# Rows of values by head, spread over the partitions as two rounded parts in place of one fp32 product

## The chip, the cores and the metric

The kernel runs on one core of a Trainium2 chip. The time is device microseconds of that core, the median of the runs shown. TensorE is called PE below (its weight loads PEld), VectorE DVE, ScalarE ACT, GpSimd POOL, SyncE SP. "Rounded" means the type fp32r: an fp32 word that TensorE takes in a shortened form. A number that is to keep its precision is then carried as two rounded words, the rounded value ("hi") and the rest ("lo").

## The reference, cut to what matters

One layer of a trunk with three parallel branches (a gated linear recurrence, gated linear attention, GLA, and an mLSTM), a merge, an output projection and a squared-ReLU MLP, for 256 prompt tokens and 8 samples of 4 tokens. The two groups are computed together: 288 columns of tokens. Three places of it concern this change; each has a number per head and token that acts on all features of the head:

```python
y_gla = rmsnorm(o.astype(dt), P['gla_g_norm']).reshape(...) * jax.nn.silu(g_gate)      # 4 heads, 256 features each
...
inter = F + m[..., None]                                                               # mLSTM, running maximum
mt = jnp.maximum(inter, jnp.max(Dm, axis=-1))
W = jnp.exp(Dm - mt[..., None])
...
y_ml = jax.nn.sigmoid(m_o) * rmsnorm(h.astype(dt), P['ml_g_norm']).reshape(B, T, MLSTM_WIDTH)
```

In the first and the last, the factor 1/sqrt(mean of squares) of a head multiplies that head's features. In the second, a running maximum of a head is subtracted within the decay matrix of the prompt part.

## The kernel before, in words

Features lie on the 128 partitions and tokens along the free axis. Every large product streams its weights: a tile of 128x1024 words comes from memory by a transfer that SP issues (`fetch`, L155), ACT rounds it into `hi` (L164), DVE subtracts to get `lo` (L171), and PE multiplies with it (`stream_`, L197 to L199): three rounded products for each 128x128 block of weights, hi by the activation's hi, hi by its lo, lo by its hi. A tile holds eight blocks, so it feeds 24 products of 128x288. There are three buffers each for the raw tile, for `hi` and for `lo`; ACT can round a new tile once PE has left the `hi` buffer that it goes into.

Beside these streams, generators called "sides" carry the branches: `run` (the loop over a stream) lets each side take one step after every weight tile. A tile scheduler with a time model then sets the order of the instructions on each engine (only SP's is by hand); code under `high_priority` is moved ahead of other work that is ready. Each engine executes its own instructions in the order so made.

A quantity per head is kept as a row block: head h stands on partitions 32h to 32h+31, all 32 alike. To let it act on a head's features it must be spread over all 128 partitions. `head_bcast` (L128) does that with one fp32 product: the stationary operand is one column of the identity, `ident[:, 32h]`, repeated 128 times, the moving operand is the row block, and the result in a PSUM tile `px` (there are two such buffers) holds row 32h on every partition. It is used in these places:

- `gla`, at the end: `inv_sqrt` makes `sums` (L498 to L502: transpose on DVE, square root on ACT, reciprocal and transpose on DVE), and for each head `scaled_rows` spreads it (L128), multiplies two blocks of features by it on DVE (L918) and splits the result into hi (ACT, L542) and lo (DVE, L543). This runs beside the stream over the mLSTM's input projection (`to_slot`, L584, evacuates that stream on ACT).
- `mlstm`, for each head: the running maximum `mr` of the 256 prompt tokens is spread, and DVE uses it from PSUM (L1406). The neighbours on PE are fp32 products (L1412, L1415).
- `mlstm`, at the end: as in `gla`, with L1582 (a gate) ahead of L918. The results `y` are the activations of the stream over `wbm`, where PE names them `s`.
- `mlstm`, once more, for 32 columns (x8 in the trace): this use stays as it is.

The kernel already has the other form in one place: `parts` (L877 to L882) rounds its source on ACT, subtracts on DVE and multiplies both parts with rounded selectors.

Of the kernel before, what the change touches and what calls it, by code (L numbers as in the profile page):

```python
# [8 lines left out]
F32 = mybir.dt.float32  # L9
F32R = mybir.dt.float32r  # L10
AF = mybir.ActivationFunctionType
ALU = mybir.AluOpType
# [41 lines left out]
def trunk(ctx, tc, io):  # L54
# [18 lines left out]
    def nm(s):  # L73
        uid[0] += 1
        return f"{s}_{uid[0]}"

    def slot(i, dt=F32):
        return big.tile([P, 8, N], dt, tag=f"s{i}", name=nm(f"s{i}"))
# [33 lines left out]
    def row(n):  # L112
        return sp.tile([P, N], F32, tag=f"r_{n}", name=nm("row"), bufs=1)
# [11 lines left out]
    def head_bcast(p, r, w=N):  # L125

        def f(h):
            T.matmul(p[:, 0:w], ident[:, 32 * h:32 * h + 1].to_broadcast([P, P]), r[:, 0:w], start=True, stop=True)  # L128
        return f


# [781 lines left out]
    def scaled_rows(y, z, r, h):  # L913

        p = misc()
        head_bcast(p, r)(h)
        a = slice(2 * h, 2 * h + 2)
        V.tensor_tensor(out=z[:, a], in0=z[:, a], in1=p[:, :N].unsqueeze(1).to_broadcast([P, 2, N]), op=ALU.mult)  # L918
        split(y[0][:, a], y[1][:, a], z[:, a])
# [6 lines left out]
        V.tensor_copy(dst[:, 2 * h:2 * h + 2, NP:N], p[:, 0:2 * NS].rearrange("p (e t) -> p e t", e=2))  # L926

    def gla():
        kk_, g_cs, ee = slot(3), slot(4), slot(5)
        wg2 = flat(kk_)[:, 4 * N:4 * N + 512]  # L930
        G.dma_start(wg2, io["wg2"])
# [193 lines left out]
        def result(h):  # L1125
            if h == 0:
                y.extend([slot(8, F32R), slot(3, F32R)])
            scaled_rows(y, sg, sums, h)

        at = {}  # L1130

        def do(s, f, *a):
            at.setdefault(s, []).append(lambda: f(*a))
# [17 lines left out]
            do(4 * h + 7, squares, h)  # L1151
            do(22 + h, result, h)
        do(20, head_sums, sums, oT)
        do(21, lambda: inv_sqrt(sums, sums, bias=eps, scale=1.0 / 256))
        yield from steps(at)
        ygla.extend(y)

# [135 lines left out]
    def mlstm():  # L1293
# [101 lines left out]
        psb = by_head(sc([P, P], "gks", 1), psb)  # L1395

        nT = slot(0)
        den = row("lf")
        cst = None
        ws = {}  # L1400
        for h in range(4):
            p = misc()
            head_bcast(p, mr, NP)(h)
            w0, w1 = ws[h] = [e0[:, 384 * h + a:384 * h + b] for a, b in ((0, 256), (256, 384))]
            for t, w in ((0, w0), (1, w1)):
                V.tensor_scalar(w, p[:, t * P:256], col[:, t, h:h + 1], 0.0, ALU.subtract, ALU.max)  # L1406
                S.activation(w, w, AF.Exp, scale=-1.0)
                V.tensor_tensor(out=w[:, 0:P], in0=w[:, 0:P], in1=C("causal"), op=ALU.mult)
            p = misc()
            for e in range(2):  # L1410
                n = 2 * h + e
                T.matmul(p[:, 0:256], mc[:, n, 0:P], tf[:, n, 0:NP], start=e == 0, stop=e == 1)  # L1412
            for e in range(2):
                n = 2 * h + e
                T.matmul(p[:, 256:384], mc[:, n, P:NP], tf[:, n, P:NP], start=e == 0, stop=e == 1)  # L1415
            V.tensor_tensor(out=w0, in0=w0, in1=p[:, 0:256], op=ALU.mult)
            V.tensor_tensor(out=w1, in0=w1, in1=p[:, 256:384], op=ALU.mult)
            yield
            if h % 2 == 0:
                cst = sp.tile([P, 1028], F32, tag="st", name=nm("st"), bufs=2)  # L1420
            for d in range(2):
                p = misc()
                for t in range(2):
                    T.matmul(p[:, 0:257], kt[:, t, h, d * P:(d + 1) * P], vt[:, t, h, :], start=t == 0, stop=t == 1)  # L1424
                o = ((h % 2) * 2 + d) * 257
                S.copy(cst[:, o:o + 257], p[:, 0:257])
            if h % 2 == 1:
                G.dma_start(io["o_C_p"][h // 2], cst)
            yield
            p = misc()  # L1430
            for e in range(2):
                for t in range(2):
                    c0 = e * 256 + t * P
                    T.matmul(p[:, c0:e * 256 + 256], vt[:, t, h, e * P:(e + 1) * P], (w0, w1)[t],  # L1434
                             start=t == 0, stop=t == 1, skip_group_check=True)
            S.copy(nT[:, 2 * h:2 * h + 2, 0:NP], p.rearrange("p (e i) -> p e i", e=2))
            if h == 3:
                p = misc()
                for t in range(2):
                    for i in range(4):  # L1440
                        T.matmul(p[32 * i:32 * i + 32, 128 * t:256], ones[:, 0:32], ws[i][t], start=t == 0, stop=t == 1, skip_group_check=True)
                V.tensor_copy(den[:, 0:NP], p[:, 0:256])
            yield
# [95 lines left out]
        def do(s, f, *a):  # L1539
            at.setdefault(s, []).append(lambda: f(*a))  # L1540
# [30 lines left out]
        do(e + 2, last)  # L1571
        do(e + 3, lambda: head_sums(sums, sqs[0]))
        do(e + 4, lambda: V.scalar_tensor_tensor(sums, sums, 1.0 / 256, den, ALU.mult, ALU.add))
        do(e + 4, lambda: inv_sqrt(sums, sums))
        yield from steps(at)
        while not mos:
            yield
# [2 lines left out]
        for h in range(4):  # L1580
            a = slice(2 * h, 2 * h + 2)
            V.scalar_tensor_tensor(nT[:, a], mo[:, a], 1.0, nT[:, a], ALU.add, ALU.mult)  # L1582
            scaled_rows(y, nT, sums, h)
            yield
        yml.extend(y)

# [268 lines left out]
```

## Time and profile before

| what | value |
|---|---|
| time, median of 3 runs | 1936.43 us (1935.52 to 1938.22) |
| the profiled execution's own time | 1936.45 us |
| its span, first to last instruction | 1934.6 us |
| granted PE clock | 0.998 |
| PE busy | 1913.4 us, 99% of the span |
| DVE / ACT / POOL busy | 53% / 42% / 13% |

The profiled execution lies 0.02 us beside the median, and 1.85 us of its time lie outside the span. Its clock is granted in full, so durations on PE can be taken as they stand. "Busy" of PE counts overlapping products once, and a product's own duration is longer than its share of the stream, since products are pipelined; what a product costs is read from the chain of work that ended last, which lists each piece from the moment the one before it let go.

### The profile page before, as it was taken

How to read it: one execution, taken by the hardware profiler on the slowest of the kernel's cores; microseconds unless marked ns; L12 is line 12 of the kernel's file. 1: busy time of each engine (PE TensorE's matmuls, PEld its weight loads, DVE VectorE, ACT ScalarE, POOL GpSimd, SP SyncE). 2: the span in 40 equal slices, each digit the busy share in tenths (PEclk: the TensorE clock that was granted, in tenths of full speed). 3: DMA queues.
4: the chain of work that ended last, by engine and by line, in shares of the span. 5: the costliest groups of instructions: out<-in, count | busy, mean ns of one | idle time of the engine just before them, and what ended most of it. 6: DMA issues, size and time to landing. Idle time of an engine off the chain costs nothing.

```text
span 1934.6 us, 35928 instructions
## 1 busy us (share of the span) xinstructions
PE 1913.4 (99%) x15068; PEld 1823.9 (94%) x15068; DVE 1032.6 (53%) x1589; ACT 805.5 (42%) x1121; POOL 242.9 (13%) x350
## 2 busy tenths in 40 slices
PE   8999999999999999999999999999999999999997
PEld 6898998999999999899999899999999999999997
DVE  6666646545673456654454654445454444444565
ACT  4333465444554344343333454443334333343433
POOL 0000100021051222001122421010000000000101
PEclk9999999999999999999999999999999999999999
DMA  9997856557443479777788464444444445444452
GB/s 385 383 353 273 308 209 237 196 202 263 159 155 112 163 226 314 270 267 273 273 328 324 137 210 159 164 164 165 167 164 170 165 154 180 165 166 168 158 175 104
DMA packets 110065, 416.42 MB, mean 215 GB/s; under 512 B 11632, under 2 KB 11808, under 8 KB 106192
## 3 DMA queue, kind: packets, MB, share of 16 engines
q1 hardware_dynamic: 100800, 381.55, 55.5%
q0 software_dynamic: 8096, 29.19, 4.3%
q10 hardware_dynamic: 1008, 3.39, 0.5%
q8 instruction: 118, 1.93, 0.4%
q14 instruction: 43, 0.35, 0.1%
HBM read 397.27 MB, written 16.81 MB: 214 GB/s over the span
## 4 chain that ended last, share of the span: by engine, by line
PE 97%; DMA 2%; DVE 1%; ACT 0%; issue 0%; SPq 0%; DVEq 0%; ACTq 0%
PE mm L197 29%; PE mm L199 28%; PE mm L198 28%; PE pa L352 4%; DMA raw<-win 1%; DMA s<-wad 1%; PE px L755 0%; DMA s<-x 0%; PE px L1511 0%; PE px L1037 0%; PE px L1424 0%; PE px L128 0%; PE pi L1495 0%; PE px L1434 0%; PE pi L1055 0%; PE pi L490 0%
## 5 line engine op out<-in xcount | busy, mean ns | idle before, releaser
L171 DVE TENSOR_TENSOR lo<-raw,hi 128x1024 fp32r<-128x1024 f32 x448 | 548.6, 1227 | 554.4 <-ACT hi L164 536.6
L164 ACT ACTIVATE hi<-raw 128x1024 fp32r<-128x1024 f32 x444 | 470.3, 1060 | 794.7 <-PE mm L198 648.9
L197 PE MATMUL mm<-xh,hi 128*128 128x288 f32 x2528 | 745.4, 299 | 0.1
L198 PE MATMUL mm<-xl,hi 128*128 128x288 f32 x2528 | 741.9, 296 | 0.0
L199 PE MATMUL mm<-xh,lo 128*128 128x288 f32 x2528 | 732.6, 296 | 0.7 <-DVE lo L171 0.6
L197 PE MATMUL mm<-s,hi 128*128 128x288 f32 x1664 | 490.5, 297 | 0.0
L197 PEld LDWEIGHTS mm<-xh,hi 128*128 128x128 f32 x2528 | 471.6, 188 | 18.8 <-issue 10.4
L198 PE MATMUL mm<-s,hi 128*128 128x288 f32 x1664 | 488.2, 295 | 0.0
L199 PE MATMUL mm<-s,lo 128*128 128x288 f32 x1664 | 477.6, 295 | 0.0
L198 PEld LDWEIGHTS mm<-xl,hi 128*128 128x128 f32 x2528 | 474.2, 188 | 1.3
L199 PEld LDWEIGHTS mm<-xh,lo 128*128 128x128 f32 x2528 | 471.2, 188 | 2.0 <-DVE lo L171 1.2
L197 PEld LDWEIGHTS mm<-s,hi 128*128 128x128 f32 x1664 | 312.0, 188 | 5.3 <-issue 5.0
L198 PEld LDWEIGHTS mm<-s,hi 128*128 128x128 f32 x1664 | 312.5, 188 | 0.2
L199 PEld LDWEIGHTS mm<-s,lo 128*128 128x128 f32 x1664 | 308.8, 188 | 0.1
L171 DVE TENSOR_TENSOR lo<-s,hi 128x1024 fp32r<-128x1024 f32 x80 | 98.0, 1225 | 113.5 <-ACT hi L164 113.5
L164 ACT ACTIVATE hi<-s 128x1024 fp32r<-128x1024 f32 x80 | 84.9, 1061 | 142.4 <-PE mm L198 141.8
L1685 POOL TENSOR_TENSOR t<-t 128x288 f32<-128x288 f32 x64 | 60.2, 951 | 639.2 <-ACT t L1684 639.2
L622 DVE TENSOR_TENSOR s<-s,mm 128x288 f32<-128x288 f32 x92 | 39.8, 451 | 44.8 <-PE mm L199 43.9
L1701 DVE TENSOR_TENSOR s<-s,mm 128x288 f32<-128x288 f32 x96 | 40.3, 450 | 33.9 <-PE mm L199 32.6
L1195 POOL TENSOR_TENSOR s<-s,t 128x288 f32<-128x288 f32 x32 | 36.4, 1165 | 174.2 <-DVE t L1194 174.2
L352 PE MATMUL pa<-s,silc 128*32 128x64 f32 (+3 forms) x832 | 49.8, 373 | 0.6 <-DMA s<-wad 0.6
L543 DVE TENSOR_TENSOR s<-t,s 128x288 fp32r<-128x288 f32 x64 | 33.8, 568 | 15.5 <-ACT s L542 15.5
(403 smaller groups left out, 1140.2 us busy)
## 6 DMA issues: line engine op xcount, KB each, us to landing
raw<-win SPq DMA_DIRECT2D x188, 512.0 KB, 4.4
raw<-wf SPq DMA_DIRECT2D x176, 512.0 KB, 4.2
s<-wf SPq DMA_DIRECT2D x80, 512.0 KB, 3.6
s<-wada SPq DMA_DIRECT2D x26, 1024.0 KB, 9.2
s<-wad SPq DMA_DIRECT2D x24, 1024.0 KB, 11.0
ag<-wada SPq DMA_DIRECT2D x22, 1024.0 KB, 5.9
raw<-wout SPq DMA_DIRECT2D x32, 512.0 KB, 5.7
st<-wada SPq DMA_DIRECT2D x20, 512.0 KB, 6.9
```

Of the source, the lines that this page charges most:

```text
L164: pace["hi"] = S.activation(hi, raw, AF.Copy)
L171: pace["lo"] = V.tensor_tensor(out=lo[:, r], in0=raw[:, r], in1=hi[:, r].bitcast(F32), op=ALU.subtract)
L197: T.matmul(pss[m][:, :N], hi[:, kk, ms], xh, start=k == k0 and not take, stop=False)
L198: T.matmul(pss[m][:, :N], hi[:, kk, ms], xl, start=False, stop=False)
L199: pace["last"] = T.matmul(pss[m][:, :N], lo[:, kk, ms], xh, start=False, stop=k == kt - 1 and keep is None)
L352: pace["prod"] = T.matmul(ps[32 * j:32 * j + 32, h * w // 4:(h + 1) * w // 4], silu_c(k), v[:, j], start=k == 0 and h == 0, stop=k == KT - ...
L543: pace["mod"] = V.tensor_tensor(out=dst_l[:, r], in0=src[:, r], in1=dst_h[:, r].bitcast(F32), op=ALU.subtract)
L622: pace["adds"].append(V.tensor_tensor(out=dst[:, base + m, :], in0=dst[:, base + m, :], in1=p, op=ALU.add))
L1195: G.tensor_tensor(out=a, in0=a, in1=t, op=ALU.add)
L1685: G.tensor_tensor(out=r, in0=r, in1=r, op=ALU.mult)
L1701: V.tensor_tensor(out=a, in0=a, in1=p, op=ALU.add)
```

## The change

The three uses of the fp32 spread with 256 or 288 columns get another form. `head_rows` rounds the row block once for all heads (`hi`, on ACT), subtracts (`lo`, on DVE), both under high priority, and returns a function that spreads one head with two rounded products into the same PSUM tile. The selector `heads_` is a rounded copy of four identity columns. The two parts lie in space that is free by then: `v2` (a slot whose rounded copies were used for the samples' states) or two row buffers.

```diff
+    heads_ = cp.tile([P, 4], F32R, tag="heads", name="heads")
+
+    def head_rows(r, to, w=N):
+
+        hi, lo = (to[:, a:a + w] for a in (0, w)) if to is not None else (sp.tile([P, N], F32R, tag=f"r_{n}", name=nm("row"), bufs=1)[:, 0:w] for n in ("ar", "rt"))
+        with tc.high_priority():
+            S.copy(hi, r[:, 0:w])
+            V.tensor_tensor(out=lo, in0=r[:, 0:w], in1=hi.bitcast(F32), op=ALU.subtract)
+
+        def f(p, h):
+            for i, a in enumerate((hi, lo)):
+                T.matmul(p[:, 0:w], heads_[:, h:h + 1].to_broadcast([P, P]), a, start=i == 0, stop=i == 1)
         return f
...
     def scaled_rows(y, z, r, h):
 
         p = misc()
-        head_bcast(p, r)(h)
+        r(p, h)
...
     def gla():
+        V.tensor_copy(heads_, ident[:, 0:P:32])
...
-            scaled_rows(y, sg, sums, h)
+            scaled_rows(y, sg, rows[0], h)
...
-        do(21, lambda: inv_sqrt(sums, sums, bias=eps, scale=1.0 / 256))
+        rows = []
+        do(21, lambda: rows.append(head_rows(inv_sqrt(sums, sums, bias=eps, scale=1.0 / 256), v2)))
...
+        mrows = head_rows(mr, None, NP)
...
-            head_bcast(p, mr, NP)(h)
+            mrows(p, h)
...
-        do(e + 4, lambda: inv_sqrt(sums, sums))
+        rows = []
+        do(e + 4, lambda: rows.append(head_rows(inv_sqrt(sums, sums), v2)))
...
-            scaled_rows(y, nT, sums, h)
+            scaled_rows(y, nT, rows[0], h)
```

The scheduler orders the changed program anew. Its order differs from the one before at these three places and hardly anywhere else; SP's order of transfers is the same row for row. Rows of the changed program carry its own line numbers: L137 is the rounding, L138 the subtraction, L142 the two rounded products, and L178, L185, L211 to L213, L516, L556, L557, L598, L932, L1294, L1300 and L1600 are the lines that were L164, L171, L197 to L199, L502, L542, L543, L584, L918, L1278, L1284 and L1582.

PE, at the end of `gla`, around the spread of the first two heads (`px` of each head; `mm` are the banks of the stream). Before:

```order
L199 MATMUL mm_5339<-xh_109,lo_5594 128x288
L128 MATMUL px_5579<-s_581_4192,con 128x288
L128 MATMUL px_5622<-s_581_4192,con 128x288
L197 MATMUL mm_5336<-xh_109,hi_5640 128x288
L198 MATMUL mm_5336<-xl_110,hi_5640 128x288
L199 MATMUL mm_5336<-xh_109,lo_5641 128x288
```

And now:

```order
L142 MATMUL px_5583<-s_630_4538,heads 128x288
L142 MATMUL px_5627<-s_630_4538,heads 128x288
L211 MATMUL mm_5339<-xh_110,hi_5646 128x288
L212 MATMUL mm_5339<-xl_111,hi_5646 128x288
L213 MATMUL mm_5339<-xh_110,lo_5647 128x288
L211 MATMUL mm_5339<-xh_110,hi_5646 128x288
L212 MATMUL mm_5339<-xl_111,hi_5646 128x288
L213 MATMUL mm_5339<-xh_110,lo_5647 128x288
L211 MATMUL mm_5340<-xh_110,hi_5646 128x288
L212 MATMUL mm_5340<-xl_111,hi_5646 128x288
L213 MATMUL mm_5340<-xh_110,lo_5647 128x288
L142 MATMUL px_5583<-s_630_4538,heads 128x288
```

The hi products of both heads stand six products of the stream later than the fp32 ones did, and the lo products nine products of the stream behind the hi ones.

DVE at the same place (L171 makes `lo` of a weight tile, L918 takes a spread head from `px`, L543 splits the result). Before:

```order
L171 TENSOR_TENSOR lo_5695<-raw_5693,hi_5694 128x1024
L918 TENSOR_TENSOR s_361_2568<-s_361_2568,px_5579 128x576
L918 TENSOR_TENSOR s_361_2568<-s_361_2568,px_5622 128x576
L171 TENSOR_TENSOR lo_5730<-raw_5728,hi_5729 128x1024
L543 TENSOR_TENSOR s_778_5578<-s_361_2568,s_777_5577 128x576 x2
L918 TENSOR_TENSOR s_361_2568<-s_361_2568,px_5673 128x576
L1278 COPY csb_5680<-px_5678 128x32
L171 TENSOR_TENSOR lo_5760<-raw_5758,hi_5759 128x1024
L543 TENSOR_TENSOR s_778_5578<-s_361_2568,s_777_5577 128x576
L1284 COPY acol_5687<-px_5682 128x16
L918 TENSOR_TENSOR s_361_2568<-s_361_2568,px_5723 128x576
L171 TENSOR_TENSOR lo_5790<-raw_5788,hi_5789 128x1024
```

And now:

```order
L185 TENSOR_TENSOR lo_5702<-raw_5700,hi_5701 128x1024
L138 TENSOR_TENSOR s_630_4538<-s_581_4194,s_630_4538 128x288
L185 TENSOR_TENSOR lo_5738<-raw_5736,hi_5737 128x1024
L932 TENSOR_TENSOR s_361_2569<-s_361_2569,px_5583 128x576
L932 TENSOR_TENSOR s_361_2569<-s_361_2569,px_5627 128x576
L557 TENSOR_TENSOR s_778_5582<-s_361_2569,s_777_5581 128x576
L185 TENSOR_TENSOR lo_5768<-raw_5766,hi_5767 128x1024
L557 TENSOR_TENSOR s_778_5582<-s_361_2569,s_777_5581 128x576
L932 TENSOR_TENSOR s_361_2569<-s_361_2569,px_5679 128x576
L1294 COPY csb_5687<-px_5685 128x32
L557 TENSOR_TENSOR s_778_5582<-s_361_2569,s_777_5581 128x576
L185 TENSOR_TENSOR lo_5798<-raw_5796,hi_5797 128x1024
```

The new subtraction stands behind the first weight tile, and the second weight tile now stands ahead of the first two heads instead of behind them.

DVE at the end of `mlstm` (L1582 is the gate of a head). Before:

```order
L502 STREAM_TRANSPOSE row_7301<-rsc_8877 128x288
L171 TENSOR_TENSOR lo_8957<-raw_8955,hi_8956 128x1024
L1582 SCALAR_TENSOR_TENSOR s_939_6775<-s_1138_8127,s_939_6775 128x576
L918 TENSOR_TENSOR s_939_6775<-s_939_6775,px_8914 128x576
L171 TENSOR_TENSOR lo_8993<-raw_8991,hi_8992 128x1024
L1582 SCALAR_TENSOR_TENSOR s_939_6775<-s_1138_8127,s_939_6775 128x576
L543 TENSOR_TENSOR s_1242_8912<-s_939_6775,s_1241_8911 128x576
L918 TENSOR_TENSOR s_939_6775<-s_939_6775,px_8950 128x576
```

And now:

```order
L516 STREAM_TRANSPOSE row_7317<-rsc_8893 128x288
L185 TENSOR_TENSOR lo_8977<-raw_8975,hi_8976 128x1024
L1600 SCALAR_TENSOR_TENSOR s_939_6783<-s_1140_8143,s_939_6783 128x576
L138 TENSOR_TENSOR s_1021_7318<-row_7317,s_1021_7318 128x288
L185 TENSOR_TENSOR lo_9014<-raw_9012,hi_9013 128x1024
L1600 SCALAR_TENSOR_TENSOR s_939_6783<-s_1140_8143,s_939_6783 128x576
L932 TENSOR_TENSOR s_939_6783<-s_939_6783,px_8932 128x576
L932 TENSOR_TENSOR s_939_6783<-s_939_6783,px_8969 128x576
```

The first two heads are taken from `px` together, behind the second weight tile and the second gate; on PE (not shown) the first head's lo product stands 16 products of the stream behind its hi product.

More of the change, by code (lines that the diff above doesn't have):

```diff
@@ L128, in f @@
             T.matmul(p[:, 0:w], ident[:, 32 * h:32 * h + 1].to_broadcast([P, P]), r[:, 0:w], start=True, stop=True)
+        return f
+    heads_ = cp.tile([P, 4], F32R, tag="heads", name="heads")
[7 more added lines that the diff above has]
+                T.matmul(p[:, 0:w], heads_[:, h:h + 1].to_broadcast([P, P]), a, start=i == 0, stop=i == 1)
         return f
```

## The prediction

> **What bounds the kernel now.** I read the busy shares first, then the chain of waits, then what PE waited for.
>
> ```profile
> PE 1913.4 (99%) x15068; PEld 1823.9 (94%) x15068; DVE 1032.6 (53%) x1589; ACT 805.5 (42%) x1121; POOL 242.9 (13%) x350
> PE 97%; DMA 2%; DVE 1%; ACT 0%; issue 0%; SPq 0%; DVEq 0%; ACTq 0%
> ```
>
> ```profile
> PE pi L556 <- DVE t L552: 6.0, 1, 6.0
> PE mm L199 <- DVE lo L171: 0.6, 1, 0.6
> ```
>
> The first row says that PE is busy for all but 1% of the span, the second that the chain that ended last runs on PE for 97% of it. The waits of PE (us in total, times, longest) name one long one, at the start of the program before any weight is multiplied, and hardly any on a weight tile's `lo`. So each microsecond that PE's stream gets shorter or longer in the middle comes off or on the end, and work on DVE (53%) and ACT (42%) costs nothing until PE waits for it. Two questions decide: what the fp32 spreads take of PE's stream and what the rounded ones will take, and whether the longer way to the row (round, subtract) or the new order makes PE wait.
>
> **What is removed.** The chain of waits around the spreads, start and length in us:
>
> ```profile
> 507.64 0.13 PE mm L199
> 507.77 0.97 PE px L128 x4
> 508.75 0.13 PE mm L197
> ...
> 511.92 0.48 PE px L128 x2
> ...
> 517.19 0.49 PE px L128 x2
> ...
> 614.66 0.28 PE px L1393 x15
> 614.94 0.63 PE px L128 x2
> ...
> 629.47 0.43 PE px L128 x2
> ...
> 658.16 0.43 PE px L128 x2
> ...
> 815.03 0.48 PE px L128 x2
> ...
> 826.07 0.48 PE px L128 x2
> ```
>
> An fp32 product is two instructions on PE: the four heads of `gla` are x4, x2 and x2. One product of 288 columns so takes 0.48 us, two instructions of 0.24. The sum: 0.97 + 0.48 + 0.49 = 1.94 us in `gla`; 4 x 0.48 = 1.92 at the end of `mlstm` (first and last of four equal pieces shown); for the running maximum, with 256 columns, 0.63 + 3 x 0.43 = 1.92 (629.47 and 658.16 are the first and last of three). Together 5.78 us. The piece of 0.63 is 0.20 longer than its three likes. It follows the fifteen tiny products of L1393, and I take the 0.20 to belong to that change of shape and to stay. Behind a spread, the stream goes on at its usual 0.13 at once (508.75), so no other price hangs on an fp32 product.
>
> **What is added on PE.** A rounded product of 288 columns has its price in the stream itself: from 504.53 to 507.73 in the rows of ACT below one weight tile passes, 3.20 us for 24 products, 0.133 each, a fresh set of weights with every one. Sixteen of them (eight heads, hi and lo) take 2.13 us. For 256 columns the kernel's own rounded selectors show the price, four neighbours in the chain:
>
> ```profile
> 684.91 0.12 PE px L881
> ...
> 685.27 0.12 PE px L882
> 685.38 0.13 PE mm L197
> ```
>
> From 684.91 to 685.38 are 0.47 us for four, 0.12 each; eight take 0.96. With the 0.20 that stays, the new form takes 2.13 + 0.96 + 0.20 = 3.29 us in place of 5.78: **2.49 us less**. Bounds: if the 0.20 goes too, 2.7 less. PE's order now has the spreads in thirteen groups (four in `gla`, four for the maximum, five at the end of `mlstm`); if the twelve others paid the 0.20 of 614.94 as well, 2.4 us, the gain would be 0.1. If rounded types brought nothing, it would be a loss (a rival below). I take 2.49, since the four L881 and L882 are the same operation, rounded selector on rounded parts, and go over into the stream at 0.13.
>
> The Trainium skill, "FP8 and Floating Point Precision", section "TensorE Precision Notes", says that a true fp32 product is four passes through the array. By that rule and a pass as long as a rounded product of the stream, a spread would take 4 x 0.133 = 0.53 us; the rows say 0.48, so the trace agrees on the order of size and is a tenth cheaper. By the rule the eight wide spreads would give 8 x (0.53 - 0.27) = 2.1 us and the four narrow ones 4 x 0.24 = 1.0, 3.1 in all, and the time would be 1933.4; I go by the rows.
>
> **What is added beside PE, and what hides it.** Per place one rounding on ACT and one subtraction on DVE; the nearest rows are the rounding in `parts` and the subtraction that makes the activations' lo:
>
> ```profile
> L877 ACT CAST t<-vs 128x256 fp32r<-128x256 f32 x4 | 1.6, 402 | 0.0
> L520 DVE TENSOR_TENSOR xl<-s,xh 128x288 fp32r<-128x288 f32 x10 | 4.5, 451 | 0.2
> ```
>
> About 0.4 us on each, three times; the copy of the selectors is a single small one on DVE. All of it lies on engines that are off the chain. It matters only where PE's order has the spread before its operands are there. In `gla`:
>
> ```profile
> 504.22 0.48 DVE L502 STREAM_TRANSPOSE s<-rsc 128x288 f32<-128x288 f32 x1
> 504.53 1.06 ACT L164 ACTIVATE hi<-raw 128x1024 fp32r<-128x1024 f32 x1 [0.59 <-PE mm L198]
> 505.62 1.23 DVE L171 TENSOR_TENSOR lo<-raw,hi 128x1024 fp32r<-128x1024 f32 x1 [0.92 <-ACT hi L164]
> ...
> 507.73 1.06 ACT L164 ACTIVATE hi<-raw 128x1024 fp32r<-128x1024 f32 x1 [2.14 <-PE mm L198]
> ```
>
> The row is there at 504.7. ACT rounds it behind the weight tile, 505.6 to 506.0. DVE subtracts behind its weight tile, 506.85 to 507.3. PE's order has the hi products six products of the stream behind 507.77, at 508.6, and the lo ones at 510.0: covers of 2.6 and 2.7 us. The running maximum's row comes from a generator (`gates`) that ends before `mlstm` starts on its heads; its rounding stands on ACT between a weight tile and two evacuations, some weight tiles ahead of 614.94, and can hold those evacuations up by its 0.4 us. At the end of `mlstm`:
>
> ```profile
> 811.78 1.06 ACT L164 ACTIVATE hi<-raw 128x1024 fp32r<-128x1024 f32 x1 [0.52 <-PE mm L198]
> ...
> 814.98 1.06 ACT L164 ACTIVATE hi<-raw 128x1024 fp32r<-128x1024 f32 x1 [2.14 <-PE mm L198]
> ...
> 828.40 0.75 DVE L543 TENSOR_TENSOR s<-s,s 128x576 fp32r<-128x576 f32 x1
> ...
> 835.99 0.30 PE L197 MATMUL mm<-s,hi 128*128 128x288 f32 x1
> ```
>
> The row is there at 812.0, rounded behind the weight tile by 813.3, subtracted behind weight tile and gate by 815.2. PE has the first hi product six products behind 815.03, at 815.8, and its lo one sixteen later, at 818.1. Covers of 2.5 and 2.9 us. What is late next: DVE takes the first head from `px` at about 818.3, where the fp32 product was done at 815.5 (815.03 and its 0.48): some 2.8 us later. The third and fourth heads keep their places on PE, so the last result stays near 829 (828.40 and its 0.75), and the stream first needs one at 835.99: 6.8 us of cover. In `gla` the results are wanted only by a much later stream.
>
> **The wait that the new order might make.** DVE and ACT execute in order, and the heads' work stands between the weight tiles. The brackets at 507.73 and 814.98 say that ACT had waited for PE to leave a `hi` buffer. With three buffers, that tile is wanted two tiles later, 6.4 us on, and its `lo` 0.27 later still. Rounding and subtracting take 1.06 + 1.23 us, so a tile may be 4.3 us late before PE waits. In `gla` the second weight tile goes ahead of the first two heads and can start as soon as its hi is there, at 508.8; the heads wait for it instead, which nobody misses. The third is rounded on ACT behind the first head's split, late by that split at most. At the end of `mlstm` the second tile goes ahead of the first head, and the third stands behind two heads taken until 819.8; its hi comes at about that time anyway. So I put this at nothing; without the cover each microsecond late is one on the end.
>
> SP's transfers keep their order, the tiles' release moves with PE, and POOL has no part in it. The two PSUM buffers of the spreads: the third head needs the first's, free about 511.1 in `gla`, and stands on PE at about 514; 3 us of cover.
>
> **Sum.** 1936.45 (the profiled execution, 0.02 beside the median of the runs) - 2.49 = **1934.0**, 0.13% less. Measurements of this kernel tell about 0.2% from no change, 3.9 us: faster is below 1932.6, slower above 1940.3. By its own working the forecast is "no change that can be told".
>
> **The rivals.**
>
> *The change of shape is paid at each group: 1936.4.* The bound above, a gain of 0.1. For it: 614.94 against its likes, and more and shorter groups than before. Against it: the stream goes on at 0.13 behind the spreads (508.75) and behind rounded selectors (685.38), and 0.63 came behind products of a quarter of the array's height, which the new groups do not follow, the first of the maximum apart. Chance 0.14.
>
> *Fp32 costs more than its rows show: 1933.4.* If the fp32 spreads hold PE for four whole passes each, part of it hidden in how the ends are modelled, 3.1 us go. For it: durations on PE overlap, and the chain's pieces are cut at modelled ends. Against it: the pieces around 507.77 add up without a gap. The page on precision, as above, gives this rule. Chance 0.10.
>
> *Weight tiles are held behind the heads: 1941.2, slower.* The place is the end of `mlstm`, on DVE. Two heads now stand in a row, both waiting for a lo product that PE has sixteen products late, and a weight tile behind them. If no tile were made from the first head to the last, 815.03 to 826.55, 11.5 us, PE would wait for what exceeds the 4.3 of cover: 7.2 us, 1934.0 + 7.2. It decides from a lateness of 4.3 us on. For it: in that order DVE has four heads and four weight tiles alternating, and ACT two splits in a row. Against it: a tile stands between the second head and the third, and between the third and the fourth, so one head's wait is all that can hold a tile. Chance 0.06.
>
> *The rounding is not taken, each part runs as fp32: 1942.2, slower.* Then 24 products at the old price stand where 12 did, 5.78 us more on 1936.45. For it: PE's rows call the operands f32 in both forms, so the type can't be read there. Against it: L881 and L882 have the same construction and cost 0.12 at 256 columns, where an fp32 product costs 0.43. Chance 0.03.
>
> **Chances and range.** The forecast has 0.67. A repeated median may lie 1 us to either side, as the runs shown do, so of it 0.11 falls below 1932.6 and the rest within. Of the four passes 0.04 falls below. Faster 0.15, same 0.14 + 0.56 + 0.06 = 0.76, slower 0.09. The range goes from 1931.5 (four passes, and 2 us of luck) to 1937.3 (the change of shape paid, and 1 us of bad luck); it leaves out the two slow cases and some 0.08 of tails.
>
> **What would show it.** In the chain of the changed kernel: spreads of 0.27 per head (0.24 for the maximum) in pieces marked L142, the stream at 0.13 right behind them, no new row of PE waiting for L137 or L138, and no longer wait for a weight tile's `lo` than 0.6. DVE's L932 of the first head near 818 at the end of `mlstm`, later than now by some 2.8, with PE busy at the same 99%. The prediction is wrong if L142 pieces cost 0.2 or more each, if PE waits for `lo` or `hi` of weights around 508 to 520 or 815 to 830, or if the span shrinks by more than 4 us, which nothing here would explain.

## The result, and the profile after

| | before | after |
|---|---|---|
| median | 1935.91 us (22 runs) | 1933.01 us (22 runs) |
| ratio, with its 95% interval | 1 | 0.9984 (0.9978 to 0.999) |
| profiled execution | 1936.45 us | 1933.03 us |
| its span | 1934.6 us | 1931.2 us |

The changed kernel is 2.9 us faster, 0.16%: less than the 0.2% at which the prediction speaks of a change, though the interval leaves out 1. One of the 22 executions took 5239.75 us, and as it was the profiled one, the profile below is that of another execution of the same kernel ("again").

First comes the busy row of the changed kernel's page; it answers to the first row of the prediction:

```profile
PE 1910.4 (99%) x15068; PEld 1822.5 (94%) x15068; DVE 1034.1 (54%) x1593; ACT 805.9 (42%) x1124; POOL 241.3 (12%) x350
```

PE executes as many instructions as before, is still busy for 99% of the span, and its busy time fell by 3.0 us. DVE has 1.5 us more and ACT 0.4. Next the chain of waits of the changed kernel around the spreads (start, length in us):

```profile
508.31 0.26 PE px L142 x2
508.58 0.13 PE mm L211
...
509.77 0.27 PE px L142 x2
...
518.20 0.27 PE px L142 x2
...
613.53 0.28 PE px L1409 x15
613.82 0.43 PE px L142 x2
...
628.18 0.24 PE px L142 x2
...
813.50 0.14 PE px L142
813.64 0.13 PE mm L211
...
815.77 0.14 PE px L142
...
819.63 0.27 PE px L142 x2
```

A head now costs 0.26 or 0.27 us in place of 0.48, and 0.24 in place of 0.43 for the maximum; the stream goes on at 0.13 right behind (508.58, 813.64). The first piece of the maximum, behind the fifteen tiny products, is 0.43, again 0.19 longer than its likes: that extra stayed, as it was before (0.63 against 0.43).

To see where the whole 3.4 us between the two profiled executions went, I took the same product of the weight stream in both traces, on either side of each place. The rows of PE's timeline (start, length, engine, line), of the kernel before:

```profile
499.93 0.30 PE L197 MATMUL mm<-xh,hi 128*128 128x288 f32 x1
...
542.01 0.29 PE L197 MATMUL mm<-xh,hi 128*128 128x288 f32 x1
...
599.92 0.29 PE L197 MATMUL mm<-xh,hi 128*128 128x288 f32 x1
...
679.95 0.29 PE L197 MATMUL mm<-s,hi 128*128 128x288 f32 x1
...
812.07 0.29 PE L197 MATMUL mm<-xh,hi 128*128 128x288 f32 x1
...
839.97 0.30 PE L197 MATMUL mm<-s,hi 128*128 128x288 f32 x1
```

and of the changed kernel:

```profile
499.67 0.30 PE L211 MATMUL mm<-xh,hi 128*128 128x288 f32 x1
...
540.87 0.29 PE L211 MATMUL mm<-xh,hi 128*128 128x288 f32 x1
...
598.79 0.29 PE L211 MATMUL mm<-xh,hi 128*128 128x288 f32 x1
...
678.04 0.29 PE L211 MATMUL mm<-s,hi 128*128 128x288 f32 x1
...
809.74 0.29 PE L211 MATMUL mm<-xh,hi 128*128 128x288 f32 x1
...
836.79 0.30 PE L211 MATMUL mm<-s,hi 128*128 128x288 f32 x1
```

From the first row to the second (`gla`) 42.08 us became 41.20: -0.88. From the third to the fourth (maximum) 80.03 became 79.25: -0.78. From the fifth to the sixth (end of `mlstm`) 27.90 became 27.05: -0.85. Together -2.5. The other 0.9 us lie where the change has no product: the first row is 0.26 early already, from the fourth to the fifth 0.42 went, and 0.24 between the sixth and the end of the span.

The same reading was made of every run. The table holds the differences from the first profile of the kernel before, in us; "wait" is the stretch from 680 to 812 (all of it after 760), "rest" what lies between the other columns, and "tail" begins at the stream's last products, at 1919. A difference of 0.01 to 0.02 is reading.

| program | to 500 | `gla` | maximum | wait | end of `mlstm` | rest | tail | span |
|---|---|---|---|---|---|---|---|---|
| before, second profile | -0.02 | 0 | -0.07 | +0.13 | 0 | 0 | 0 | 1934.7 |
| changed (again) | -0.27 | -0.87 | -0.78 | -0.40 | -0.85 | -0.01 | -0.25 | 1931.2 |
| changed, third profile | -0.58 | -0.87 | -0.78 | -0.53 | -0.85 | -0.01 | -0.24 | 1930.8 |
| `gla` alone | -0.58 | -0.87 | -0.07 | -0.35 | 0 | -0.01 | -0.26 | 1932.5 |
| maximum alone | -0.71 | -0.01 | -0.78 | -0.53 | 0 | -0.01 | -0.24 | 1932.4 |
| end of `mlstm` alone | -0.47 | -0.01 | -0.07 | -0.38 | -0.85 | -0.01 | -0.26 | 1932.6 |
| both parts in fp32 | -0.60 | +1.93 | +1.69 | -0.53 | +1.89 | -0.01 | -0.25 | 1938.8 |
| before, fp32 spreads eight times | +0.02 | +13.57 | +12.09 | +0.02 | +13.55 | +0.93 | 0 | 1974.8 |
| changed, rounded spreads eight times | +0.05 | +6.54 | +5.72 | +0.28 | +6.59 | +0.03 | -0.24 | 1953.6 |
| subtraction eight times | -0.28 | -0.90 | -0.78 | -0.20 | -0.46 | -0.01 | -0.25 | 1931.8 |
| hi alone | -0.63 | -1.39 | -1.13 | -0.51 | -1.39 | +0.01 | -0.26 | 1929.4 |
| changed, sums rounded | -0.29 | -0.87 | -0.78 | -0.53 | -0.85 | -1.39 | -0.75 | 1929.2 |

Two profiles of the same program agree to 0.1 us at the three places. The -0.07 of three rows at the maximum stands at one product of the stream, at 679.95 before, behind the spreads, where the first profile of the kernel before is that much later than these three. The 0.93 of the eightfold fp32 kernel in "rest" lies far from its products: 0.74 of it stands at one product, for which PE waits 0.48 us for the `lo` of a weight tile that had landed late.

### The profile page after: what moved, and what is told of

The parts are those of the page before. It is cut to its first block, busy times and chain, and to the rows that moved or that the text cites. A ratio compares the mean times of both kernels' runs of the same rounds, so it can differ in the third digit from the quotient of the medians.

```text
span 5237.9 us, 35934 instructions
## 1 busy us (share of the span) xinstructions
PE 5219.9 (100%) x15068; PEld 4706.9 (90%) x15068; DVE 1050.0 (20%) x1593; ACT 818.0 (16%) x1124; POOL 212.2 (4%) x350
## 3 DMA queue, kind: packets, MB, share of 16 engines
q8 instruction: 118, 1.93, 0.2%
## 4 chain that ended last, share of the span: by engine, by line
PE 100%; DVE 0%; DMA 0%; DVEq 0%; ACT 0%; issue 0%; SPq 0%
PE mm L211 29%; PE mm L212 29%; PE mm L213 29%; PE pa L366 5%; PE px L769 1%; PE px L1052 1%; PE px L1528 0%; PE px L1441 0%; PE pi L1512 0%; PE pi L1070 0%; PE mm L250 0%; PE mm L249 0%; PE mm L248 0%; PE px L1451 0%; PE pi L1065 0%; PE px L1126 0%
## 5 line engine op out<-in xcount | busy, mean ns | idle before, releaser
L211 PE MATMUL mm<-xh,hi 128*128 128x288 f32 x2528 | 1560.6, 622 | 0.0
L212 PE MATMUL mm<-xl,hi 128*128 128x288 f32 x2528 | 1559.8, 618 | 0.0
L213 PE MATMUL mm<-xh,lo 128*128 128x288 f32 x2528 | 1539.1, 617 | 0.0
L211 PEld LDWEIGHTS mm<-xh,hi 128*128 128x128 f32 x2528 | 975.3, 386 | 105.3 <-issue 61.0
L213 PEld LDWEIGHTS mm<-xh,lo 128*128 128x128 f32 x2528 | 985.8, 391 | 49.7 <-issue 6.0
L212 PEld LDWEIGHTS mm<-xl,hi 128*128 128x128 f32 x2528 | 983.6, 389 | 47.4 <-issue 9.6
L185 DVE TENSOR_TENSOR lo<-raw,hi 128x1024 fp32r<-128x1024 f32 x448 | 547.4, 1223 | 2286.5 <-ACT hi L178 2286.1
L211 PE MATMUL mm<-s,hi 128*128 128x288 f32 x1664 | 964.6, 580 | 0.0
L212 PE MATMUL mm<-s,hi 128*128 128x288 f32 x1664 | 962.9, 579 | 0.0
L178 ACT ACTIVATE hi<-raw 128x1024 fp32r<-128x1024 f32 x444 | 469.4, 1057 | 3106.2 <-PE mm L212 2908.0
L213 PE MATMUL mm<-s,lo 128*128 128x288 f32 x1664 | 942.6, 577 | 0.0
L211 PEld LDWEIGHTS mm<-s,hi 128*128 128x128 f32 x1664 | 616.4, 370 | 27.3 <-issue 16.3
L212 PEld LDWEIGHTS mm<-s,hi 128*128 128x128 f32 x1664 | 614.9, 370 | 11.7 <-issue 2.0
L213 PEld LDWEIGHTS mm<-s,lo 128*128 128x128 f32 x1664 | 612.7, 370 | 12.8 <-issue 1.2
L185 DVE TENSOR_TENSOR lo<-s,hi 128x1024 fp32r<-128x1024 f32 x80 | 97.9, 1224 | 412.8 <-ACT hi L178 412.8
L178 ACT ACTIVATE hi<-s 128x1024 fp32r<-128x1024 f32 x80 | 84.6, 1058 | 509.8 <-PE mm L212 509.8
```

The costliest lines, as they stand in the source:

```text
L178: pace["hi"] = S.activation(hi, raw, AF.Copy)
L185: pace["lo"] = V.tensor_tensor(out=lo[:, r], in0=raw[:, r], in1=hi[:, r].bitcast(F32), op=ALU.subtract)
L211: T.matmul(pss[m][:, :N], hi[:, kk, ms], xh, start=k == k0 and not take, stop=False)
L212: T.matmul(pss[m][:, :N], hi[:, kk, ms], xl, start=False, stop=False)
L213: pace["last"] = T.matmul(pss[m][:, :N], lo[:, kk, ms], xh, start=False, stop=k == kt - 1 and keep is None)
```

## The experiments

### One place at a time

These runs are the changed kernel again, and three kernels with the new form left at one place only; the selectors' copy and tile stay in all. For `gla` alone:

```diff
-        mrows = head_rows(mr, None, NP)
+        mrows = lambda p, h: head_bcast(p, mr, NP)(h)
...
-        do(e + 4, lambda: rows.append(head_rows(inv_sqrt(sums, sums), v2)))
+        do(e + 4, lambda: rows.append((lambda r: lambda p, h: head_bcast(p, r)(h))(inv_sqrt(sums, sums))))
```

The maximum alone has the second of these edits and the same at the end of `gla`:

```diff
-        do(21, lambda: rows.append(head_rows(inv_sqrt(sums, sums, bias=eps, scale=1.0 / 256), v2)))
+        do(21, lambda: rows.append((lambda r: lambda p, h: head_bcast(p, r)(h))(inv_sqrt(sums, sums, bias=eps, scale=1.0 / 256))))
```

The end of `mlstm` alone has that one and the first.

> The changed kernel once more, for a profile whose rows can be set beside those of before, and for its difference on one chip. Price theory (only the products' own cost moved): 2.5 to 2.7 us below the kernel before; spreads of 0.27 us a head in the chain (0.24 for the maximum), the stream at 0.13 behind them, no new wait of PE. Order theory (the new order on DVE and ACT removes waits of PE as well): more than 2.7 below, and the stream's pieces between the heads are shorter in sum than before. Shape theory (each group of spreads pays 0.20 for the change of shape): groups of two products cost 0.4 or more, and a gain above 2 could not come from the spreads.

> The rounded parts at the end of the attention branch alone, fp32 spreads at the two other places; the same is computed. Price theory: 1.94 - 8 x 0.133 = 0.9 us below the kernel before. Order theory: this is the place where a weight tile moved ahead of the heads, so it would hold most of the gain, 1.5 or more. Shape theory: four groups pay 0.8, nothing is left, 0 to 0.1.

> The rounded parts for the running maximum alone; the same is computed. Price theory: 1.72 - 0.96 = 0.8 us below the kernel before, 1.0 if the first piece's extra 0.20 goes too. Order theory: 0.8, as the order hardly moves here. Shape theory: 0 to 0.2.

> The rounded parts at the end of the mLSTM branch alone; the same is computed. Price theory: 1.92 - 8 x 0.133 = 0.9 us below the kernel before. Order theory: between 0.9 and 1.5. If weight tiles were held behind the heads here, no gain or a loss. Shape theory: five groups pay 1.0, nothing is left.

Measured beside 33 runs of the kernel before (1936.25 us) on the same chip: again 1932.80 (ratio 0.9982, 0.9973 to 0.999); `gla` alone 1934.50 (0.9992, 0.9983 to 1.0001); maximum alone 1934.99 (0.9994, 0.9984 to 1.0003); end of `mlstm` alone 1934.47 (0.999, 0.9982 to 0.9999). The gain of all three, 3.45, is above the 2.5 to 2.7 of the price theory, and each single gain is above its 0.8 or 0.9 too, as the order theory would have it; the interval of a ratio is some 1.7 us to either side, so these times alone decide nothing. The table does: each place gives its 0.8 to 0.9 us where it is and at most 0.07 at the other two, so no place gains more than its products' price. The three gains in time, 1.75, 1.26 and 1.78, add up to 4.8, more than the 3.45 of all three together. That fits a part that every one of these programs has once, whichever place it changes, of (4.8 - 3.45) / 2 = 0.7 us. The table shows such a part: to 500, in the wait and in the tail.

### The prices

Three kernels repeat or replace products. In the kernel before each spread with 256 or 288 columns is made eight times:

```diff
-            T.matmul(p[:, 0:w], ident[:, 32 * h:32 * h + 1].to_broadcast([P, P]), r[:, 0:w], start=True, stop=True)
+            for _ in range(8 if w >= NP else 1):
+                T.matmul(p[:, 0:w], ident[:, 32 * h:32 * h + 1].to_broadcast([P, P]), r[:, 0:w], start=True, stop=True)
```

> The kernel before with each wide fp32 spread done eight times in a row into the same buffer; the last one counts, so the result is the same. 84 products more, 56 of 288 columns and 28 of 256. By the rows of the chain: 56 x 0.483 + 28 x 0.43 = 39.1 us more than the kernel before. By four passes of a rounded product's price: 56 x 0.53 + 28 x 0.48 = 43.1. If the chain's pieces hide part of the cost, still more.

In the changed kernel each pair of rounded products is made eight times:

```diff
-            for i, a in enumerate((hi, lo)):
+            for i, a in list(enumerate((hi, lo))) * 8:
```

> The changed kernel with each pair of rounded products done eight times in a row into the same buffer; the result is the same. 84 pairs more. By the rows of the stream and of the rounded selectors: 56 x 0.267 + 28 x 0.235 = 21.5 us more than the changed kernel, so about 18.6 more than the kernel before. If alternating products were dearer than the stream's (0.2 each), 84 x 0.4 = 33.6 more than the changed kernel.

And in the changed kernel both parts go through PE as fp32:

```diff
-                T.matmul(p[:, 0:w], heads_[:, h:h + 1].to_broadcast([P, P]), a, start=i == 0, stop=i == 1)
+                T.matmul(p[:, 0:w], heads_.bitcast(F32)[:, h:h + 1].to_broadcast([P, P]), a.bitcast(F32), start=i == 0, stop=i == 1)
```

> The changed kernel with both parts and the selectors given to the array as fp32; the row is still rounded and subtracted, and the same is computed. Price theory: 24 fp32 products where the kernel before had 12, so 5.6 us above the kernel before and some 8.3 above the changed kernel. If the change's gain came from the order on DVE and ACT and not from the price of the products, it would stay within 1 or 2 us of the changed kernel.

Measured beside 17 runs of the kernel before (1936.18): 1976.06 (1.0208, 1.0193 to 1.0223), 1954.74 (1.0095, 1.0078 to 1.0112) and 1941.54 (1.0027, 1.0016 to 1.0037). That is 39.9, 18.6 and 5.4 us more, where 39.1, 18.6 and 5.6 were expected from the prices. The chain of waits with eight fp32 products (two instructions each, four heads here and there in one piece):

```profile
507.79 7.76 PE px L129 x32
...
628.53 3.65 PE px L129 x16
...
646.10 3.45 PE px L129 x16
```

and with eight rounded pairs:

```profile
523.32 2.13 PE px L142 x16
...
621.54 2.06 PE px L142 x16
...
637.51 1.87 PE px L142 x16
```

An fp32 product of 288 columns costs 7.76 / 16 = 0.485 us, of 256 columns 3.45 / 8 = 0.431. A rounded one costs 2.13 / 16 = 0.133 and 1.87 / 16 = 0.117. The stages of the table say the same: the 28 products more in `gla` (seven for each of four heads) cost 13.57 / 28 = 0.485, and the 28 pairs more, against the changed kernel, (6.54 + 0.87) / 28 = 0.265. Both first pieces of the maximum are longer by the same 0.20 (3.65 - 3.45, 2.06 - 1.87), once for eight products or pairs in a row. So the extra stands at the first piece behind the tiny products, whichever form comes; that the tiny products are its cause fits all of these, and was not tried apart.

The spreads of the kernel with fp32 parts, by line, from its trace (ns shortest, median, longest; first and last start):

```profile
L142 PE MATMUL px<-s,heads x32: 403/405/407, 507.8 to 830.5; 128*128 128x288 f32 x32
L142 PE MATMUL px<-row,heads x16: 377/379/482, 616.2 to 661.3; 128*128 128x256 f32 x16
```

and the same of the changed kernel:

```profile
L142 PE MATMUL px<-s,heads x16: 290/296/375, 508.1 to 823.1; 128*128 128x288 f32 x16
L142 PE MATMUL px<-row,heads x8: 281/284/382, 613.7 to 656.5; 128*128 128x256 f32 x8
```

The operands are called f32 in both, but the fp32 form has twice the instructions and each is longer. With the same rounding, subtraction and tiles, nearly the same order (on PE some spreads stand up to nine products of the stream earlier) and only the products' type put back, the kernel is 8.7 us slower than the changed one, which was measured on another chip, and 5.4 slower than the kernel before (1941.54 against 1932.80 and 1936.18; the three places alone give +5.51). So the gain at the three places comes from the type of the products; neither the rounding and subtraction nor the new order brings any of it.

### The cover of the subtraction

The subtraction on DVE, eight times:

```diff
-            V.tensor_tensor(out=lo, in0=r[:, 0:w], in1=hi.bitcast(F32), op=ALU.subtract)
+            for _ in range(8):
+                V.tensor_tensor(out=lo, in0=r[:, 0:w], in1=hi.bitcast(F32), op=ALU.subtract)
```

> The changed kernel with each of the three subtractions done eight times over; the result is the same. 21 subtractions more, 21 x 0.45 = 9.5 us on DVE, 3.2 us at each place, a little more than the 2.7 to 2.9 us of cover that the prediction works out for lo at the two normalisations. If DVE's work there is covered: within 1 us of the changed kernel (2.9 below the kernel before), since what exceeds the cover is 0.3 to 0.5 a place. If DVE's work at these places were on the path: up to 9.5 us above the changed kernel.

Measured: 1933.60 (0.9988, 0.9978 to 0.9997), 0.8 us above the changed kernel's 1932.80 of another chip; the spans of the two profiles differ by 0.5. At `gla` and the maximum nothing was lost (-0.90 and -0.78). At the end of `mlstm` -0.46 stands in place of -0.85: 0.39 us lost. DVE's timeline there and, in the second fence, the chain of waits:

```profile
812.51 1.43 DVE L139 TENSOR_TENSOR s<-row,s 128x288 fp32r<-128x288 f32 x3
...
823.02 1.42 DVE L933 TENSOR_TENSOR s<-s,px 128x576 f32<-128x576 f32 x2 [1.27 <-PE px L143]
```

```profile
822.85 0.27 PE px L143 x2
...
832.99 0.21 ACT s L1193
```

The scheduler put weight tiles between the eight subtractions and moved the lo products on PE behind them, so that DVE took the first head at 823.0, some 7 us later than in the changed kernel (815.94, below). PE never waited for the row. What it waited for is an evacuation on ACT (L1193) of the stream ahead, which has nothing to do with the spreads. PE's timeline has the place, the first product of the heads' own stream, and DVE's, in the last row, the last head's `lo`:

```profile
832.79 0.29 PE L214 MATMUL mm<-xh,lo 128*128 128x288 f32 x1
833.25 0.40 PE L212 MATMUL mm<-s,hi 128*128 128x288 f32 x1 [0.16 <-ACT s L1193]
...
832.07 0.75 DVE L558 TENSOR_TENSOR s<-s,s 128x576 fp32r<-128x576 f32 x1
```

The two products start 0.46 us apart, where the stream goes at 0.13, and set product by product against the changed kernel the whole loss stands at this one place. ACT's timeline of this kernel shows why the evacuation is late:

```profile
830.80 0.67 ACT L557 ACTIVATE s<-s 128x576 fp32r<-128x576 f32 x1
831.49 1.28 ACT L1193 ACT_TABLE_LOAD   x1
```

and of the changed kernel:

```profile
824.19 0.69 ACT L556 ACTIVATE s<-s 128x576 fp32r<-128x576 f32 x1
...
830.80 1.28 ACT L1192 ACT_TABLE_LOAD   x1
```

The split of the last head (L557) now ends right ahead of a table load of 1.28 us, and the load with the evacuations behind it begins 0.69 us later (831.49 against 830.80; L1193 there is L1192 here). So the cover is there at all three places, and it is smallest at the end of `mlstm`: there 7 x 0.45 = 3.2 us more on DVE begin to cost. What runs out first there is not the time until the heads' own stream, which the prediction had counted, but the room on ACT ahead of that table load. The other was nearly gone too: the last head's `lo` is done at 832.82, and by the stream's pace the first product was due at 832.92.

### One rounded part

Left out is the lo part: no subtraction, and one product for each head.

```diff
-            V.tensor_tensor(out=lo, in0=r[:, 0:w], in1=hi.bitcast(F32), op=ALU.subtract)
...
-            for i, a in enumerate((hi, lo)):
-                T.matmul(p[:, 0:w], heads_[:, h:h + 1].to_broadcast([P, P]), a, start=i == 0, stop=i == 1)
+            T.matmul(p[:, 0:w], heads_[:, h:h + 1].to_broadcast([P, P]), hi, start=True, stop=True)
```

> The changed kernel without the lo part: one rounded product a head, no subtraction. It leaves out the correction of the rounded rows, so its outputs are coarser; the time is what is looked at. Price theory: 8 x 0.133 + 4 x 0.12 = 1.5 us below the changed kernel, 4.0 at the three places below the kernel before. If the group's change of shape or the wait for lo were the price and not the product: less than 0.8 or more than 2 below the changed kernel.

Measured: 1931.44 (0.9976, 0.9966 to 0.9985), 1.4 us less than the changed kernel's 1932.80; at the three places 0.52 + 0.35 + 0.54 = 1.41, where eight products of 0.133 and four of 0.117 make 1.53. The 0.12 that is missing stands at the maximum, and not at the heads: product by product each head saves 0.117 there, and one piece of the stream behind the last of them, at 678, is 0.15 longer. So 1.5 us is what the second part costs; the subtraction beside it costs nothing that can be seen.

### The part that no place explains

Each of the two kernels was profiled once more, to see whether the 0.9 us outside the three places is luck of one execution.

> The kernel before, one more profile. In the first profiles, set stream product by stream product, the changed kernel gained 2.48 us at the three places, and 0.26 before the first 40 us and 0.43 around 798 us besides, where the change has no part. If these two are the luck of one execution (when transfers land), this profile differs from the first one of before by as much, within 0.7 us at the start and 0 to 0.5 around 798, and by nothing (0.05) at the three places. If they belong to the kernel, the start and the wait around 798 are again those of the first profile.

> The changed kernel, one more profile. At the three places again 2.4 to 2.5 us less than before, to 0.05 us. If the start and the stretch around 798 are luck, they differ from the other profile of this kernel by some tenths; if they belong to the kernel, PE has no wait around 796 again.

They gave 1936.48 and 1932.58. The second profile of the kernel before has the stretches outside as the first had them, within 0.13; the third of the changed kernel has them 0.4 lower still. So it isn't the luck of one execution, though some tenths move from one to the next, and the programs part into two families: all with the new selectors' tile are early at 500 (the eightfold rounded one apart), and have a tail shorter by 0.24 or more; the two of the old form, the eightfold one among them, have neither. The kernel with both parts in fp32 belongs to the first family, so it is not the shorter products.

What happens in the wait stretch can be read. The kernel before, in the order of time on ACT, DVE and PE's weight loads:

```profile
795.03 1.06 ACT L164 ACTIVATE hi<-raw 128x1024 fp32r<-128x1024 f32 x1 [4.69 <-DMA raw<-win]
...
797.27 1.65 DVE L1514 SCALAR_TENSOR_TENSOR s<-s,csb,px 128x256 f32<-128x256 f32 x4
...
798.19 0.30 PEld L1511 LDWEIGHTS px<-s,s 128*128 128x128 f32 x2 [0.35 <-DVE s L1514]
```

The changed kernel:

```profile
792.69 1.06 ACT L178 ACTIVATE hi<-raw 128x1024 fp32r<-128x1024 f32 x1 [7.25 <-DMA raw<-win]
...
794.92 1.65 DVE L1531 SCALAR_TENSOR_TENSOR s<-s,csb,px 128x256 f32<-128x256 f32 x4
...
795.84 0.30 PEld L1528 LDWEIGHTS px<-s,s 128*128 128x128 f32 x2
```

A weight tile (`raw<-win`) lands late in both, since ACT waits for it. Behind it on DVE stands the decay work of L1514, and PE's product L1511 waits for that, 0.35 us, in the kernel before. ACT has the tile at 795.03 before and at 792.69 after, 2.34 us earlier, where PE's stream was only 1.9 us earlier (679.95 to 678.04, and 0.02 more by 760): the 0.4 us decide, and the wait is gone. In the tail, the stores of the output on ACT's queue land in the median after 3.1 us before (first row, the transfers by issue) and after 2.7 in the changed kernel (second):

```profile
o_y<-s ACTq DMA_DIRECT2D x2, 288.0 KB, 3.1
```

```profile
o_y<-s ACTq DMA_DIRECT2D x2, 288.0 KB, 2.7
```

Every program with the new tile shows 2.7 there, and the two of the old form 3.1. So transfers that the change doesn't touch land earlier. Why is open. What the programs of the first family have in common is the new tile (16 bytes of each partition), its copy on DVE, and the rounding of a row at one place or more; which of them matters was not tried. The wait stretch is no clean sign of it, since the eightfold rounded kernel has the tile and lost 0.28 there.

### The same exchange at another place

The sums of squares (L504) are fp32 products with a matrix of ones, two instructions each. In this kernel, on top of the change, those for the last four blocks of features take the squares as one rounded part, with rounded ones; what was summed on POOL stays fp32.

```diff
+    ones_r = cp.tile([P, P], F32R, tag="ones_r", name="ones_r")
+    V.tensor_copy(ones_r, ones)
...
-        sq = t288()
+        sq = t288() if k <= KT - 5 else t288(F32R)
...
-                pace["sum"] = T.matmul(ps[:, :N], ones, lasts.pop(0), start=False, stop=not lasts)
+                pace["sum"] = T.matmul(ps[:, :N], ones_r, lasts.pop(0), start=False, stop=not lasts)
```

> The changed kernel, and in the two sums of squares over all features (the RMS norms behind the output projection and at the end) the squares of the last four blocks go as one rounded part each, with rounded ones, in place of four fp32 products; it leaves out the lo part of these squares. By the prices shown, 4 x (0.485 - 0.133) = 1.4 us less of PE at each of two places. At the end of the program ACT makes the squares 0.4 apart, so the last product alone is left behind the last square and about 0.8 to 1.0 of the 1.4 comes off the end. In all 1.5 to 2.6 us below the changed kernel, 4.4 to 5.5 below the kernel before. If these products are hidden behind the squares anyway: 0.5 at most.

Measured: 1931.12 (0.9974, 0.9965 to 0.9984), 5.1 us less than the kernel before in the same runs, 1.7 to 1.9 less than the changed kernel's two medians, which were measured in other runs. It is the fastest kernel of this study. The table puts 1.4 us of it between 840 and 1919, the price of four products, and 0.5 in the tail, where 0.8 to 1.0 was expected. In the changed kernel's chain four fp32 products there are one piece, the first row; in this kernel's, the second, only the last products still stand on the chain behind a square on ACT:

```profile
1916.94 2.44 PE pi L504 x8
```

```profile
1916.09 0.45 ACT t L497
1916.59 0.75 PE pi L506 x2
```

The end of the kernel gained less than the products' price: there the last two products can't start before the last square (L497) is done.

## Why the prediction was right, and where it was not

- **What bounds the kernel.** PE's stream: right. What was taken off the stream at a place came off the span (the three single kernels, the eightfold ones and hi alone, each with its price times its count).
- **What is removed, 5.78 us.** Right. The eightfold kernel puts the fp32 product at 0.485 and 0.431 us, the forecast had 0.48 and 0.43 from the chain.
- **The 0.20 that stays.** Right: 0.43 against 0.24 in the changed kernel, and once for eight in the eightfold ones. (The tiny products of L1393 have the form 128*32 in the trace: all rows of the array and a quarter of its columns, where the prediction speaks of its height. Nothing hangs on it.)
- **What is added, 2.13 + 0.96 us.** Right: 0.265 for a pair and 0.24, in every group, no matter how short, but for the 0.20 just named.
- **The three places together, 2.49 us.** Right: 2.50 measured, and 2.43 against the second profile of the kernel before.
- **Covers on ACT and DVE.** Right at each. The subtraction in the changed kernel, by line (ns, first and last start), and then the first head at the end of `mlstm` from DVE's timeline:

```profile
L138 DVE TENSOR_TENSOR s<-s,s x1: 452/452/452, 506.5 to 506.5; 128x288 fp32r<-128x288 f32 x1
...
L138 DVE TENSOR_TENSOR s<-row,s x1: 450/450/450, 812.4 to 812.4; 128x288 fp32r<-128x288 f32 x1
```

```profile
815.94 1.42 DVE L932 TENSOR_TENSOR s<-s,px 128x576 f32<-128x576 f32 x2 [0.30 <-PE px L142]
```

In `gla` the subtraction ends at 506.95 and PE takes hi at 508.31 and lo behind it; at the end of `mlstm` it ends at 812.85 and PE takes lo at 815.77. No row of PE waits for L137 or L138. The first head is taken at 815.94, where 818.3 was foretold on the old time scale; the stream was 2.33 us earlier by then (812.07 to 809.74), which makes 816.0. The lateness of 2.7 us was free, as foretold: the last head's `lo` is done at 826.0, 6.8 us ahead of the stream that needs it.

- **Weight tiles held behind the heads (1941.2).** Did not happen. The longest wait of PE for a weight tile's `lo` is the old one, in the waits of PE (us, times, longest):

```profile
PE mm L213 <- DVE lo L185: 0.6, 1, 0.6
```

- **Change of shape paid at each group (1936.4).** Fell: the pieces of one product (813.50) cost 0.14, and eight pairs in a row cost no less per pair than a pair alone.
- **Fp32 costs four whole passes (1933.4).** Its time is the nearest of all to the medians, by luck, and it fell all the same: the eightfold kernel gives 0.485 / 0.133 = 3.6 rounded products of 288 columns, and 0.431 / 0.117 = 3.7 of 256, for an fp32 product, and the three places show 2.5 us and not 3.1. The Trainium skill, "FP8 and Floating Point Precision", section "TensorE Precision Notes", counts four passes for it. An estimate by that rule, four at 0.133, would have made the 28 products more in `gla` cost 14.9 us; 13.57 were measured, so as a price it is a tenth too high here.
- **The rounding is not taken (1942.2).** Fell: with both parts put to PE as fp32 the kernel takes 1941.54.
- **The sum, 1934.0.** The median was 1933.01, 1.0 us lower and within the range. Rather more than half of that is where the sum starts: 1936.45 lay beside the median of 3 runs, and 22 runs of the kernel before gave 1935.91. The rest is the gain, 2.90 us between the two medians (3.45 beside the runs of "again") in place of 2.49. The three terms were right, so the weak step is the last one, that 1936.45 less the three terms is the time: it holds everything else of the program fixed, and the text says that SP's transfers keep their order. They did, but some landed earlier, at the start, around 790 and at the end; that was put at nothing and measured -0.9 in the profile that is compared and -1.3 in another. Nothing on record gives its sign or size ahead of time, and its cause is open. That the result is "no change that can be told" by 0.2% came out as forecast.

## What to carry to other kernels

Where PE's stream is the bound, an fp32 product with a selector can be replaced by two rounded products of its parts at 55% of the price (0.265 against 0.485 us at 288 columns), as long as a rounding and a subtraction of one row find room on other engines a few microseconds ahead. Count such a gain from the pieces of the chain, not from the durations of single products (290 to 296 ns for a rounded one that costs 133). And a microsecond in two thousand may come or go elsewhere with a new program: a gain of that size is shown by the same product of the stream in both traces, place by place, not by the total.

## What the runs showed that I had not expected

Every program with the new selectors' tile (four words per partition) and its copy differs from the kernel before by 0.7 to 1.5 us outside the places that were changed, at the start, at one weight tile and in the last stores, and does so even where the products stay fp32; the one with the rounded spreads eight times is the exception, with a loss of 0.1 in all. The cause is open.
